# The first layer's input projections by one level of Strassen's scheme

## The chip, the core and the metric

The kernel runs on one core of a Trainium2 chip. The metric is the device time of one execution in microseconds (us). TensorE (PE in the profile) multiplies, with its weight loads (PEld) beside the products; VectorE (DVE), ScalarE (ACT) and GpSimd (POOL) work on elements; SyncE (SP) issues all DMAs of this kernel, in order. Each engine executes its own instructions in program order.

## The reference, cut to what matters

Two layers over 2048 tokens of width 1024. The change touches the first, a stick-breaking attention layer with 16 heads of 64:

```python
proj = rms_norm(x, norm_g) @ w_in          # (2048 x 1024) @ (1024 x 4096)
q, k, v, gate = jnp.split(proj, 4, axis=-1)
# per block of 128 queries:
z = q . k * scale
log_fail = where(mask, log_sigmoid(-z), 0)
later = reverse_cumsum(log_fail) - log_fail
a = where(mask, exp(log_sigmoid(z) + later), 0)
o = a @ v
x = x + (o * silu(gate)) @ w_out
```

The second layer is latent attention with a softmax; nothing of it is changed. Products are in single precision: every operand is split into a high part (as the matmul reads it) and the rest, and three products of parts (`HLS`) stand for one.

## The kernel before

**Stages of layer one.** The work goes by head pairs (`hp`, 8 of them) and, within one, by token groups (`j`, 4 of 512 tokens): 32 stages. `proj0(n)` projects stage n; `attn0(hp, j)` is its attention. The program writes `attn0` of a stage and then `proj0` of the next, whose priorities are spread over the attention's, so that the products of the next stage fill PE's waits of this one.

**A projection** has four units (q, k, v, gate), each 128 outputs by 512 tokens in one PSUM bank (`pj`): 8 blocks of 128 inputs times 3 products of parts, so 24 matmuls of 512 columns, 96 for a stage. Activations come as tiles `xn` (512 KB, high and low part), loaded from the scratch `xn_d` in every pair but the first; in the first, the normed x is turned on PE, scaled by the gain, split and written there (`norm_scale`, `norm_turn`). Weights (`w`, high and low) stay for the four stages of a pair; in the last one each unit's successor is loaded in pieces (`wraw`) and split by ACT and POOL (`load_w`). Then q is split into `qd`, k into `ks`, v is copied, turned and split into `vv`, and the gate becomes `gt`.

**Attention** goes head by head (2 in a pair), over key groups g = j to 0, and over 4 row tiles of 128 queries. A row tile is: 2 matmuls into `z`, two sigmoids on ACT, a scan on DVE (`pp`), a product on POOL (`a`), up to 4 turns on PE (`t`), the split into `at` by ACT and DVE (a subtraction), and 2 matmuls of `av` on average. So DVE has one scan and one subtraction in each row tile, POOL one product and small copies. Where g = j, a row tile has 128 to 512 keys; elsewhere 512. Rings: 3 banks for z, 3 buffers for pp, 5 for a.

**What sets the order.** A list scheduler in the program (`Sched.issue`) places each engine's instructions by modelled durations, then by priority; the order on each engine is fixed from then on. The chip only waits where an operand is late.

Of the kernel before, what the change touches and what calls it, by code (L numbers as in the profile page):

```python
# [11 lines left out]
F32 = mybir.dt.float32  # L12
# [370 lines left out]

@with_exitstack
def trunk(ctx: ExitStack, tc: tile.TileContext, x, w0, wo0, g0, g1, wlat, wgate, gqa, gkva,
# [23 lines left out]
    xn_d = scratch([NG, KD, P, 2, G], "xn_d")  # L409
    y_d = scratch([NG, P, HP0, 2, G], "y_d")  # L410
# [60 lines left out]

    def norm_turn(xts, gain, dst, j, tag=None):
# [28 lines left out]
    XB = KD + 2  # L501
    ws, kv, xq, cur = {}, {}, {}, {}

    def load_w(hp, u, early=None):
        w = pw.tile([P, 2, KD, P], F32R, "w", 4)
        for n, raw in enumerate(early or ()):
            k = slice(4 * n, 4 * n + 4)
            split_sb(w[:, 0, k], w[:, 1, k], raw, 4 * P, "dve" if n else "pool")
        if early:
            ws[hp, u] = w  # L510
            return
        for k in range(0, KD, 2):
            raw = pw.tile([P, 2, P], F32, "wraw", 4)
            C.dma(raw, w0[hp, u, :, k:k + 2, :], 128)
            split_sb(w[:, 0, k:k + 2], w[:, 1, k:k + 2], raw, 2 * P)
        ws[hp, u] = w

    def xn_tile():
        return pw.tile([P, 2, G], F32R, "xn", XB)

    def load_xn(hp, j, k):
        t = xn_tile()
        C.dma(t.all().bitcast(F32), xn_d[j, k], 512)
        xq[hp, j, k] = t

    def load_x(j):
        if j < 2:
            xt = pa.tile([P, 4, D], F32, "at", 2)
            xts = [xt[:, i, :] for i in range(4)]
        else:  # L530
            xts = [pk.tile([P, D], F32, ("ks", "vv")[i % 2], 5).all() for i in range(4)]
        for i in range(4):
            C.dma(xts[i], x[(4 * j + i) * P:(4 * j + i + 1) * P, :], 512)
        return xts

    def xn_dst(j):
        def dst(k):
            xq[0, j, k] = xn_tile()
            return xq[0, j, k]
        return dst  # L540

    stages = [(hp, j) for hp in range(HP0) for j in range(NG)]

    def proj0(n):
        hp, j = stages[n]
        nxt = stages[n + 1] if n + 1 < len(stages) else None

        def mul(u, after=None):
            acc = bank("pj")
            w = ws[hp, u]  # L550
            unit(acc, lambda a, k: w[:, a, k, :], lambda k, b: xq[hp, j, k][:, b, :], after=after)
            if j == NG - 1 and hp + 1 < HP0:
                load_w(hp + 1, u)
            return acc

        acc = mul(0)
        qd = pk.tile([P, 2, 2, G], F32R, "qd", 2)
        for h in range(2):
            lo_, hi_ = slice(64 * h, 64 * h + 64), slice(64 - 64 * h, 128 - 64 * h)
            split(qd[lo_, h, 0, :], qd[lo_, h, 1, :], acc[lo_, :])  # L560
            C.dma(qd[hi_, h].bitcast(F32), qd[lo_, h].bitcast(F32), 256)
        acc = mul(1)
        ks = pk.tile([P, 2, G], F32R, "ks", 5)
        for h in range(2):
            lo_, hi_ = slice(64 * h, 64 * h + 64), slice(64 - 64 * h, 128 - 64 * h)
            split(ks[lo_, h, :], ks[hi_, h, :], acc[lo_, :])
        acc = mul(2)
        vt = pa.tile([P, G], F32, "tmp", 2)
        C.act(vt, acc, AF.Copy)
        tb = bank("pj")  # L570
        with sched.group():
            for c in range(4):
                C.turn(tb[:, c * P:(c + 1) * P], vt[:, c * P:(c + 1) * P], ident)
# [3 lines left out]

        def ahead(k):
            if nxt and nxt[0] > 0:
                if k == 0:  # L580
                    for e in range(XB - KD):
                        load_xn(*nxt, e)
                if k + XB - KD < KD:
                    load_xn(*nxt, k + XB - KD)

        acc = mul(3, ahead)
        sg = pa.tile([P, G], F32, "tmp", 2)
# [59 lines left out]
    x0 = load_x(0)  # L647
    C.dma(gsb0, g0, 4)
    C.dma(gsb1, g1, 4)
    load_w(0, 0)  # L650
    early = {}
    for u in range(1, 4):
        early[u] = []
        for n in range(2):
            if u < 3:
# [3 lines left out]
            raw = raw.rearrange("p (k d) -> p k d", k=4)  # L659
            C.dma(raw, w0[0, u, :, 4 * n:4 * n + 4, :], 256)  # L660
            early[u].append(raw)
    nextx = load_x(1) if NG > 1 else None
    norm_scale(pa, x0, "tmp", 2, True)
    norm_turn(x0, gsb0, xn_dst(0), 0)
    C.fill(later[:, 0:G - P], 0.0)
    causal(later[:, G - P:G], -1, 1.0)
    for u in range(1, 4):
        load_w(0, u, early[u])
    if NG > 1:
        norm_scale(pa, nextx, "tmp", 2)  # L670
    proj0(0)
# [20 lines left out]
    for n, (hp, j) in enumerate(stages):  # L692
# [3 lines left out]
        if n + 1 < len(stages):  # L696
            if hp == 0 and j + 1 < NG:
                norm_turn(nextx, gsb0, xn_dst(j + 1), j + 1, "pj")
            proj0(n + 1)
            late = len(sched.ops)  # L700
            if hp == 0 and j + 2 < NG:
                nextx = load_x(j + 2)
                norm_scale(pa, nextx, "tmp", 2)
# [457 lines left out]
```

## Time and profile before

| | us |
|---|---|
| median of 3 runs (3061.26 to 3068.74) | 3061.82 |
| the profiled execution | 3061.58 |
| its span, first to last instruction | 3059.9 |
| layer one: first row tile to the end of its attention | 39 to 1588 |
| one pair in the regular part (second to seventh) | 187.0 |

A span's busy shares are means over very different stretches. The regular part of layer one repeats itself with 187.0 us from pair to pair, so that one pair can be read for six. Busy time of PE counts matmuls that overlap in the pipeline; what a matmul costs in a row of them is the distance of starts. The same holds on DVE: its instructions of 512 columns follow one another some 80 ns sooner than their ends say.

### The profile page before, as it was taken

What the parts mean: (1) busy time and instruction counts of PE and PEld (TensorE: products, weight loads), DVE (VectorE), ACT (ScalarE), POOL (GpSimd) and SP (SyncE); (2) the same over time, 40 slices, a digit from 0 to 9 for tenths busy, and PEclk for the clock granted to TensorE, in tenths of its full rate; (3) what the DMA queues carried; (4) which work ended last, traced back from release to release, by engine and by line L of the source; (5) the groups of instructions that cost most, each with busy time, mean ns of one, the idle gap of its engine ahead of it and who ended that gap; (6) DMA issues with size and microseconds to landing.
All of it is one profiled execution on the core that took longest, in us unless ns stands there. A gap on an engine that the chain in (4) does not pass through costs nothing.

```text
span 3059.9 us, 48542 instructions
## 1 busy us (share of the span) xinstructions
PE 2978.5 (97%) x15728; PEld 2486.1 (81%) x15728; DVE 2024.9 (66%) x3553; ACT 1865.3 (61%) x4635; POOL 1491.4 (49%) x2931
## 2 busy tenths in 40 slices
PE   8899999999999999999999999999999999999999
PEld 6678888888888888888778888878888888888787
DVE  5777896978868778787863231047778777778511
ACT  5676786867768677786852132247777776777400
POOL 4664664756647565574652120136456455555200
PEclk9899999999999999999999999999999999999999
DMA  6253334344243342433339673142222232223462
GB/s 241 104 172 124 130 105 140 109 138 148 81 152 103 125 152 83 150 112 115 126 122 324 243 274 117 69 158 83 78 92 72 86 104 66 75 78 93 160 219 103
DMA packets 134797, 399.87 MB, mean 131 GB/s; under 512 B 16656, under 2 KB 39696, under 8 KB 131984
## 3 DMA queue, kind: packets, MB, share of 16 engines
q1 hardware_dynamic: 134544, 396.76, 38.3%
q8 instruction: 126, 2.06, 0.3%
q14 instruction: 127, 1.04, 0.1%
HBM read 272.97 MB, written 98.57 MB: 121 GB/s over the span
## 4 chain that ended last, share of the span: by engine, by line
PE 75%; DVE 11%; ACT 7%; issue 3%; POOL 2%; DMA 2%; POOLq 0%; DVEq 0%; ACTq 0%; SPq 0%
PE pj L297 30%; PE z L297 21%; PE av L297 12%; PE t L301 9%; DVE pp L342 3%; PE t L297 3%; DVE at L319 1%; DVE pt L319 1%; PE pj L301 1%; ACT s L312 1%; ACT a L312 1%; DVE qs L329 1%; DVE y L319 1%; DVE nm L349 1%; ACT j L312 1%
## 5 line engine op out<-in xcount | busy, mean ns | idle before, releaser
L297 PE MATMUL pj<-xn,w 128*128 128x512 f32 x3072 | 863.6, 402 | 2.0 <-DVE qd L319 1.9
L319 POOL TENSOR_TENSOR a<-a,pp 128x512 f32<-128x512 f32 (+3 forms) x640 | 611.6, 958 | 474.0 <-DVE pp L342 437.4
L297 PEld LDWEIGHTS pj<-xn,w 128*128 128x128 f32 x3072 | 545.4, 188 | 100.0 <-issue 3.7
L342 DVE TENSOR_TENSOR_SCAN pp<-z,cy,a 128x512 f32<-128x512 f32 x384 | 484.1, 1273 | 43.8 <-ACT z L312 39.8
L312 ACT ACTIVATE at<-t 128x512 fp32r<-128x512 f32 (+3 forms) x640 | 340.8, 535 | 156.7 <-PE t L301 154.6
L319 DVE TENSOR_TENSOR at<-t,at 128x512 fp32r<-128x512 f32 (+3 forms) x640 | 377.8, 599 | 84.4 <-ACT at L312 79.5
L312 ACT ACTIVATE a<-z 128x512 f32<-128x512 f32 (+3 forms) x640 | 335.5, 535 | 115.7 <-PE z L297 93.0
L297 PE MATMUL z<-ks,qd 128*128 128x512 f32 (+3 forms) x1280 | 365.2, 377 | 13.7 <-DVE pp L342 9.0
L297 PE MATMUL av<-at,vv 128*128 128x512 f32 (+3 forms) x1280 | 376.1, 379 | 2.1 <-DVE at L319 2.1
L301 PE MATMUL t<-ident,a 128*128 128x128 f32 x2176 | 343.6, 274 | 8.9 <-POOL a L319 4.3
L301 PEld LDWEIGHTS t<-ident,a 128*128 128x128 f32 x2176 | 271.6, 141 | 83.3 <-POOL a L319 7.9
L312 ACT ACTIVATE z<-z 128x512 f32<-128x512 f32 (+3 forms) x640 | 338.7, 536 | 0.7
L329 POOL TENSOR_SCALAR s<-s,c,ri 128x512 f32<-128x512 f32 (+3 forms) x280 | 200.9, 729 | 172.9 <-DVE ri L360 128.1
L297 PEld LDWEIGHTS z<-ks,qd 128*128 128x128 f32 x1280 | 225.2, 190 | 66.6 <-DVE pp L342 20.9
L297 PE MATMUL av<-pt,vv 128*128 128x512 f32 (+2 forms) x960 | 266.3, 384 | 5.0 <-DVE pt L319 3.9
L297 PE MATMUL z<-knt,qn 128*128 128x512 f32 (+2 forms) x960 | 256.8, 376 | 12.1 <-ACT s L312 11.8
L312 ACT ACTIVATE s<-z,nm 128x512 f32<-128x512 f32 (+2 forms) x320 | 199.8, 627 | 102.7 <-DVE nm L349 68.0
L297 PEld LDWEIGHTS av<-at,vv 128*128 128x128 f32 x1280 | 223.1, 190 | 38.0 <-DVE at L319 5.5
L319 DVE TENSOR_TENSOR pt<-t,pt 128x512 fp32r<-128x512 f32 (+1 forms) x312 | 184.3, 606 | 98.6 <-ACT pt L312 96.5
L342 DVE TENSOR_TENSOR_SCAN pp<-z,later 128x128 f32<-128x128 f32 (+3 forms) x256 | 204.3, 814 | 46.8 <-ACT z L312 28.5
L312 ACT ACTIVATE pt<-t 128x512 fp32r<-128x512 f32 (+1 forms) x312 | 163.3, 536 | 72.6 <-PE t L301 70.3
L297 PEld LDWEIGHTS z<-knt,qn 128*128 128x128 f32 x960 | 160.4, 189 | 35.8 <-ACT s L312 17.9
(234 smaller groups left out, 4945.5 us busy)
## 6 DMA issues: line engine op xcount, KB each, us to landing
xn<-xn_d SPq DMA_DIRECT2D x224, 512.0 KB, 4.7
xn_d<-xn SPq DMA_DIRECT2D x64, 512.0 KB, 3.8
y_d<-yh SPq DMA_DIRECT2D x64, 512.0 KB, 2.6
y<-y_d SPq DMA_DIRECT2D x60, 512.0 KB, 5.1
qd<-qd SPq DMA_DIRECT2D x64, 256.0 KB, 3.1
xk<-xn_d SPq DMA_DIRECT2D x32, 512.0 KB, 6.1
cqt<-c_d SPq DMA_DIRECT2D x16, 1024.0 KB, 5.0
ckv<-c_d SPq DMA_DIRECT2D x32, 512.0 KB, 3.7
```

The lines of the kernel that those rows point to most:

```text
L297: lambda: self.nc.tensor.matmul(R(out), lhsT=R(l), rhs=R(r), start=start, stop=stop),
L301: self.s.add("pe", 109.0, lambda: self.nc.tensor.transpose(R(out), R(src), R(ident)), refs(out), refs(src, ident))
L312: self.nc.scalar.activation(R(out), R(src), func, **kw)
L319: self.s.add(eng, ns, lambda: self.eng[eng].tensor_tensor(out=R(out), in0=R(a), in1=R(b), op=op), refs(out), refs(a, b))
L329: self.s.add(eng, ns, lambda: self.eng[eng].tensor_scalar(out=R(out), in0=R(a), scalar1=R(s1), scalar2=R(s2), op0=op0, op1=op1), refs(out) ...
L342: lambda: self.nc.vector.tensor_tensor_scan(R(out), R(a), R(b), initial=R(init), op0=ALU.mult, op1=op),
L349: lambda: self.nc.vector.tensor_reduce(out=R(out), in_=R(src), axis=AX.X, op=op, **kw),
```

## The change

One level of Strassen's scheme, in its form with seven products (Winograd's), on blocks: the 1024 inputs are halved, the 512 tokens of a group are halved, and of the four units two pairs are formed (q with k, v with gate), of which each pair's two units are the halves of the outputs. Of eight products of blocks, seven are left, each with 512 inputs, 128 outputs and 256 tokens; both unit pairs share a PSUM bank. A stage has 7 x 4 x 2 x 3 = 168 matmuls of 256 columns.

- Weights: seven combinations for each unit pair (`WB`), four of them sums or differences. In the first pair they are formed by DVE and POOL (`first_w`); for the later ones `load_w` loads the raw blocks for each combination anew (56 pieces of 128 KB where 16 were), forms the sums on POOL, and splits 28 pieces where it split 16.
- Activations: seven combinations (`XBL`) of two 512 KB tiles (`xs`), so 14 where 8 were. In the first pair they are summed by POOL and DVE (`make_x`), turned, split and written to `xs_d`; in the later ones they are loaded, through a ring of 4 (`XB`, before 10).
- Gain: multiplied onto x in its rows (`gain_scale`), so that it needs a row of gains over all partitions, made at the start; before, it was a scale in the split.
- Results: the products are summed from PSUM into `c1` and `c2` in SBUF: one ACT copy and seven DVE sums a stage. `qd` and `ks` are then split from there; the product with the gate's sigmoid goes from DVE to POOL.

```diff
-    XB = KD + 2
+    XB = 4
+    H = G // 2
+    PAIR = ((0, 1), (2, 3))
...
+    def load_w(hp, s):
+        for p, (ua, ub) in enumerate(PAIR):
+            w = w_tile()
+            for n in range(2):
...
+                b = WB[s]
+                if b[0] == "A":
+                    t = raw(b)
+                else:
+                    t = raw("A21") if b != "S3" else raw("A11")
+                    other = raw("A22") if b != "S3" else raw("A21")
+                    C.tt("pool", t, t, other, ALU.add if b != "S3" else ALU.subtract, H)
+                    if b in ("S2", "S4"):
+                        C.tt("pool", t, t, raw("A11"), ALU.subtract, H)
+                    if b == "S4":
+                        C.tt("pool", t, raw("A12"), t, ALU.subtract, H)
+                split_sb(w[:, 0, ks_], w[:, 1, ks_], t, 2 * P)
...
+    def gain_scale(pl, xts, grow, mixed=False):
...
+            if mixed and i % 2 == 0:
+                C.act(xts[i], xts[i], AF.Copy, D, scale=r)
+                C.tt("pool", xts[i], xts[i], grow, ALU.mult, D)
+            else:
+                C.stt(xts[i], xts[i], r, grow, ALU.mult, ALU.mult, D)
...
+        for s in range(7):
+            if hp == 0:
+                make_x(j, s, xh)
             acc = bank("pj")
...
+                        for p in range(2):
+                            for m, (a, b) in enumerate(HLS):
+                                C.mm(acc[:, p * H:(p + 1) * H], ws[hp, p, s][:, a, k, :], xt[:, kk, b, :],
+                                     k == 0 and m == 0 and p == 0, k == 3 and m == 2 and p == 1, H)
             if j == NG - 1 and hp + 1 < HP0:
-                load_w(hp + 1, u)
+                load_w(hp + 1, s)
+            if s == 0:
+                C.act(c1[:, :, 1, :], av_, AF.Copy)
+            elif s == 1:
+                C.tt("dve", c1[:, :, 0, :], av_, c1[:, :, 1, :], ALU.add)
...
-        C.act(sg, acc, AF.Sigmoid)
         gt = pa.tile([P, G], F32, "gt", 2)
-        C.tt("dve", gt, acc, sg, ALU.mult)
+        C.act(gt, g_, AF.Sigmoid)
+        C.tt("pool", gt, g_, gt, ALU.mult)
```

**How the order moves.** PE, in the attention of the fifth pair's last token group, shortly after its first key groups. `pj<-xn,w` (`pj<-xs,w` in the changed kernel) are matmuls of the next projection, `z`, `t` and `av` those of the attention. Before:

```order
L297 MATMUL z<-ks,qd 128x512 x2
L297 MATMUL pj<-xn,w 128x512 x6
L301 MATMUL t<-ident,a 128x128 x4
L297 MATMUL z<-ks,qd 128x512 x2
L297 MATMUL pj<-xn,w 128x512 x3
L301 MATMUL t<-ident,a 128x128 x4
L297 MATMUL z<-ks,qd 128x512 x2
L297 MATMUL pj<-xn,w 128x512 x3
```

And in the changed kernel, at the same row tiles:

```order
L301 MATMUL t<-ident,a 128x128 x8
L297 MATMUL z<-ks,qd 128x512 x2
L297 MATMUL av<-at,vv 128x512 x4
L301 MATMUL t<-ident,a 128x128 x4
L297 MATMUL av<-at,vv 128x512 x2
L297 MATMUL z<-ks,qd 128x512 x2
L297 MATMUL av<-at,vv 128x512 x2
L301 MATMUL t<-ident,a 128x128 x4
```

Before, three or six projection matmuls stand between any two row tiles. In the changed kernel there is none from the 57th to the 79th of that pair's 80 row tiles (46 matmuls of z): the projection that could fill stands complete ahead of them.

POOL, in the fifth pair's third token group, where the weights of the next pair are made: `a<-a,pp` is a row tile's product, `w<-wraw,w` the split of a weight piece, `wraw<-wraw` a sum of two. Before:

```order
L319 TENSOR_TENSOR w<-wraw,w 128x256 x2
L319 TENSOR_TENSOR a<-a,pp 128x512
L364 COPY cy<-pp 128x1
L364 COPY pp<-cy 128x1
L364 COPY cy<-pp 128x1
L319 TENSOR_TENSOR a<-a,pp 128x512
```

And in the changed kernel:

```order
L319 TENSOR_TENSOR w<-wraw,w 128x256 x2
L364 COPY pp<-cy 128x1
L364 COPY cy<-pp 128x1
L319 TENSOR_TENSOR a<-a,pp 128x512
L319 TENSOR_TENSOR wraw<-wraw 128x256
L364 COPY pp<-cy 128x1
L364 COPY cy<-pp 128x1
L319 TENSOR_TENSOR a<-a,pp 128x512
L319 TENSOR_TENSOR wraw<-wraw 128x256 x2
L364 COPY pp<-cy 128x1
```

A row tile's product now has one to three weight instructions behind it; all 56 of a pair stand among the 24 row tiles of the third token group.

DVE, at the start, up to the first scan of the program. `xn` and `xs` are activation splits, `c_` the sums of products, `at` (without `t`) sums of x. Before, 24 instructions stand ahead of the first scan, of which these are the last:

```order
L336 SCALAR_TENSOR_TENSOR tmp,nss<-at 128x1024 x2
L319 TENSOR_TENSOR qd<-pj,qd 64x512 x2
L319 TENSOR_TENSOR ks<-pj,ks 64x512 x2
L319 TENSOR_TENSOR vv<-pj,vv 128x4x128
L336 SCALAR_TENSOR_TENSOR xn<-pj,gsb_91,xn 128x512
L342 SCALAR_TENSOR_TENSOR pp<-z,later 128x128
```

In the changed kernel, 65 instructions stand ahead of it, and its last are:

```order
L319 TENSOR_TENSOR qd<-c_281,qd 64x512 x2
L319 TENSOR_TENSOR vv<-pj,vv 128x4x128
L319 TENSOR_TENSOR c_518<-c_518,pj 128x2x256
L319 TENSOR_TENSOR at<-at 128x512
L319 TENSOR_TENSOR xs<-pj,xs 128x2x256
L319 TENSOR_TENSOR ks<-c_518,ks 64x512 x2
L319 TENSOR_TENSOR tmp<-at 128x512
L319 TENSOR_TENSOR xs<-pj,xs 128x2x256
L342 SCALAR_TENSOR_TENSOR pp<-z,later 128x128
```

Ahead of the first scan stand now 46 element instructions of 512 columns (8 before, and 9 gain splits), 10 of 1024 columns (4 and 2 scalings before) and 8 of 128.

## Rows read from the trace of the kernel before

**Rows 1.** The page: span, then busy us, share and instructions by engine.

```profile
span 3059.9 us, 48542 instructions
PE 2978.5 (97%) x15728; PEld 2486.1 (81%) x15728; DVE 2024.9 (66%) x3553; ACT 1865.3 (61%) x4635; POOL 1491.4 (49%) x2931
```

**Rows 2.** Windows, second and seventh pair: length, busy by engine, clock, DMA.

```profile
277.03:464.05 187.02, 186.35 (x994) 155.00 (x993) 150.26 (x197) 138.97 (x296) 114.85 (x260) 1.00 0.37 125
...
1212.14:1399.20 187.06, 186.44 (x994) 154.99 (x993) 150.59 (x197) 138.93 (x296) 114.85 (x260) 1.00 0.37 122
```

**Rows 3.** Waits, layer one: who for whom, us in all, times, longest.

```profile
POOL a L319 <- DVE pp L342: 437.4, 289, 15.2
```

**Rows 4.** Timeline of PE, 278 to 284: start, us, instructions.

```profile
279.08 3.63 PE L297 MATMUL pj<-xn,w 128*128 128x512 f32 x15
282.55 0.60 PE L301 MATMUL t<-ident,a 128*128 128x128 f32 x4
282.91 0.94 PE L297 MATMUL pj<-xn,w 128*128 128x512 f32 x3
283.69 0.27 PE L301 MATMUL t<-ident,a 128*128 128x128 f32 x1
```

**Rows 5.** Timeline of PE in layer two, where matmuls have 256 columns.

```profile
2136.54 1.59 PE L297 MATMUL pj<-wukv,ckv 128*128 128x256 f32 x12
2137.97 0.45 PE L297 MATMUL z<-knt,qn 128*128 128x128 f32 x3
```

**Rows 6.** Groups of DVE in one pair: count, busy us, mean ns, idle before.

```profile
L319 DVE TENSOR_TENSOR at<-t,at 128x512 fp32r<-128x512 f32 x56 | 37.6, 678 | 6.8 <-ACT at L312 6.4
...
L319 DVE TENSOR_TENSOR y<-y,gt 128x512 f32<-128x512 f32 x4 | 3.1, 768 | 0.0
...
L319 DVE TENSOR_TENSOR gt<-pj,tmp 128x512 f32<-128x512 f32 x4 | 2.7, 683 | 0.0
```

**Rows 7.** Timeline of DVE in the last pair's last token group.

```profile
1538.05 0.66 DVE L319 TENSOR_TENSOR at<-t,at 128x512 fp32r<-128x512 f32 x1
1538.63 1.27 DVE L342 TENSOR_TENSOR_SCAN pp<-z,cy,a 128x512 f32<-128x512 f32 x1
1539.82 0.71 DVE L319 TENSOR_TENSOR wo<-woraw,wo 128x256 fp32r<-128x256 f32 x1
```

**Rows 8.** Windows, the same attention, which has no projection beside it.

```profile
1530.00:1560.00 30.00, 27.58 (x146) 21.55 (x145) 29.47 (x41) 27.41 (x66) 25.62 (x55) 1.00 0.28 85
```

**Rows 9.** Groups of POOL in one pair.

```profile
L319 POOL TENSOR_TENSOR a<-a,pp 128x512 f32<-128x512 f32 x56 | 61.2, 1094 | 35.2 <-DVE pp L342 33.3 <-ACT at L312 1.0 <-ACT a L312 0.3
L319 POOL TENSOR_TENSOR w<-wraw,w 128x256 fp32r<-128x256 f32 x16 | 12.1, 761 | 2.6 <-ACT w L312 2.5
...
L364 POOL COPY cy<-pp 128x1 f32<-128x1 f32 x48 | 8.8, 183 | 2.4 <-DVE pp L342 1.3 <-ACT at L312 1.1
...
L319 POOL TENSOR_TENSOR a<-a,pp 128x256 f32<-128x256 f32 x8 | 5.1, 638 | 12.8 <-DVE pp L342 12.7
```

**Rows 10.** Timeline of DVE at the start.

```profile
5.80 1.23 DVE L336 SCALAR_TENSOR_TENSOR tmp<-at 128x1024 bf16<-128x1024 f32 x1 [5.80 <-DMA at<-in_x_dram]
...
20.01 3.40 DVE L319 TENSOR_TENSOR w<-a,w 128x512 fp32r<-128x512 f32 x2
23.34 0.68 DVE L319 TENSOR_TENSOR w<-pp,w 128x512 fp32r<-128x512 f32 x1
...
39.16 0.75 DVE L336 SCALAR_TENSOR_TENSOR xn<-pj,gsb,xn 128x512 fp32r<-128x512 f32 x1 [1.53 <-ACT xn L312]
40.91 0.42 DVE L342 TENSOR_TENSOR_SCAN pp<-z,later 128x128 f32<-128x128 f32 x1 [1.01 <-ACT z L312]
```

**Rows 11.** Windows, first pair from its first scan, and a stretch in it.

```profile
40.00:262.00 222.00, 208.01 (x1061) 165.93 (x1060) 163.35 (x218) 152.78 (x321) 126.91 (x276) 0.95 0.41 143
...
80.00:90.00 10.00, 4.97 (x15) 2.46 (x14) 8.31 (x11) 8.11 (x18) 9.36 (x16) 0.70 0.13 52
```

**Rows 12.** Loads of xn, 277 to 1399: us from issue to landing.

```profile
DMA to landing us min/median/max: 3.0/4.7/7.2
```

More of the change, by code (lines that the diff above doesn't have):

```diff
@@ L526, in load_x, with xs_tile @@
+    def xs_tile():
+        return pw.tile([P, 2, 2, H], F32R, "xs", XB)
     def load_x(j):
         if j < 2:
[L528 to L531 removed]
+            xt = pa.tile([P, 4, 2, G], F32, "at", 2)
+            halves = [[xt[:, i, h, :] for h in range(2)] for i in range(4)]
+            whole = [xt[:, i].rearrange("p a b -> p (a b)") for i in range(4)]
+        else:
+            tiles = [pk.tile([P, 2, G], F32, ("ks", "vv")[i % 2], 5) for i in range(4)]
+            halves = [[t[:, h, :] for h in range(2)] for t in tiles]
+            whole = [t.all().rearrange("p a b -> p (a b)") for t in tiles]
@@ L532, in load_x @@
         for i in range(4):
[L533 to L540, printed above, removed]
-    stages = [(hp, j) for hp in range(HP0) for j in range(NG)]
-    def proj0(n):
-        hp, j = stages[n]
-        nxt = stages[n + 1] if n + 1 < len(stages) else None
-        def mul(u, after=None):
-            acc = bank("pj")
-            w = ws[hp, u]
-            unit(acc, lambda a, k: w[:, a, k, :], lambda k, b: xq[hp, j, k][:, b, :], after=after)
-            if j == NG - 1 and hp + 1 < HP0:
-                load_w(hp + 1, u)
[L554 to L562, printed above, removed]
+            C.dma(whole[i], x[(4 * j + i) * P:(4 * j + i + 1) * P, :], 512)
@@ new lines, in load_x, with make_x @@
+        return whole, halves
+    t2s = {}
+    def make_x(j, s, xh):
+        b = XBL[s]
+        eng = ("pool", "dve")
+        if b == "T2":
+            for i in range(2):
+                C.tt(eng[i], xh[i][0], xh[i + 2][0], xh[i][0], ALU.subtract)
+                t2s[i] = pa.tile([P, G], F32, "tmp", 2)
+                C.tt(eng[i], t2s[i], xh[i + 2][1], xh[i][0], ALU.subtract)
+        elif b == "T3":
+            for i in range(2):
+                C.tt(eng[i], xh[i + 2][0], xh[i + 2][1], xh[i + 2][0], ALU.subtract)
+        elif b == "T4":
+            for i in range(2):
+                C.tt(eng[i], xh[i][1], t2s[i], xh[i][1], ALU.subtract)
+        src = {"B11": lambda i: xh[i][0], "B21": lambda i: xh[i][1], "B22": lambda i: xh[i + 2][1],
+               "T1": lambda i: xh[i][0], "T2": lambda i: t2s[i][:, :], "T3": lambda i: xh[i + 2][0],
+               "T4": lambda i: xh[i][1]}[b]
+        for hb in range(2):
+            tb = bank("pj" if j else ("z", "t", "z", "t", "z", "av")[(2 * s + hb) % 6])
+            with sched.group():
+                for kk in range(2):
+                    for i in range(2):
+                        k, o = 2 * hb + kk, (2 * kk + i) * P
+                        C.turn(tb[:, o:o + P], src(i)[:, k * P:(k + 1) * P], ident)
+            t = xs_tile()
+            split(t[:, :, 0, :], t[:, :, 1, :], tb.all().rearrange("p (k t) -> p k t", k=2))
+            C.dma(xs_d[j, 2 * s + hb], t.all().bitcast(F32), 512)
+            xq[j, 2 * s + hb] = t
@@ L576, in proj0 @@
         split(vv[:, :, 0::3, :], vv[:, :, 1:3, :], tv)
[L578 to L587, printed above, removed]
-        C.act(sg, acc, AF.Sigmoid)
         gt = pa.tile([P, G], F32, "gt", 2)
-        C.tt("dve", gt, acc, sg, ALU.mult)
+        g_ = c2[:, 1].rearrange("p a t -> p (a t)")
+        C.act(gt, g_, AF.Sigmoid)
+        C.tt("pool", gt, g_, gt, ALU.mult)
         kv[hp, j] = (ks, vv)
```

155 lines of the change are left out of this document (111 added, 44 removed).

## The prediction

> **What bounds the kernel now.** The page first: PE is busy 97% of the span, DVE 66%, ACT 61%, POOL 49% [rows 1]. Those are means, so the windows come next: layer one repeats with 187.0 us a pair, in which PE is busy 186.4, DVE 150.3 to 150.6, ACT 139 and POOL 114.9, at a full clock [rows 2]. PE is the limit there, and DVE has only 36 us to spare in a pair. The waits say the same from the other side: POOL waits 437 us for DVE's scans [rows 3], the longest of all in layer one, and PE's sums are small beside that. But where attention has no projection beside it, the limit is another: in the last pair's last token group DVE is busy 29.5 of 30 us and PE 27.6 by its modelled ends [rows 8]. So a projection does two things here: it costs PE time, and it fills the time in which attention waits for DVE. What the change saves is worth something only while both hold.
>
> **Fewer columns on PE.** Fifteen matmuls of 512 columns take 282.55 - 279.08 = 3.47 us, 0.231 each [rows 4]; twelve of 256 columns in a row take 1.43, 0.119 each [rows 5], so half the columns cost 52%, weight loads included. A stage had 96 x 0.231 = 22.2 us and has 168 x 0.119 = 20.0: 2.2 less, 8.6 in a pair, 69 in 32 stages. With PE alone a pair would take 187.0 - 8.6 = 178.4.
>
> **Work added to DVE.** A pair gets 28 sums from PSUM and loses 4 gate products. A subtraction of 512 columns is followed by the next instruction after 0.58 [rows 7], and the gate product (one operand in PSUM, one in SBUF, as the new sums) lasts as long as a subtraction, 683 against 678 ns [rows 6]. So 24 x 0.6 = 14.4: DVE rises from 150.5 to 165, 92% of 178.4. That would still fit if it were spread evenly. It isn't. In the last token group's attention the new order has 23 row tiles (57th to 79th) with no projection matmul between them. Of their 22 intervals, 18 are of 512 keys and 4 on the diagonal (128 to 512 keys, mean 320). DVE needs 0.58 + 1.19 = 1.77 for a scan and a subtraction [rows 7]: 18 x 1.77 + 4 x 1.77 x 320/512 + 2 x 0.6 (for y) = 37.5. PE needs for such a row tile 4 matmuls and 4 turns. A turn is (283.69 - 282.55 - 3 x 0.231)/4 = 0.11 [rows 4], so a row tile is 1.36, and the stretch 18 x 1.36 + 4 x 0.85 = 27.9. PE waits for 9.6; less some 1.6 for the row tile by which it can lead with three banks of z: 8. Its bounds are 5 (a lead of three row tiles) and 10. So 178.4 + 8 = 186.4: nearly the whole saving is given back to DVE.
>
> **Work added to POOL.** In a pair, 12 more weight splits at 0.76, 28 sums of 256 columns, for which the product of 256 columns at 0.64 is the nearest row, and 4 gate products at 1.09 [rows 9]: 9.1 + 17.9 + 4.4 = 31, so 114.9 becomes 146, 82% of 178. All 56 weight instructions stand among the third token group's 24 row tiles, so POOL has there 28 x 0.76 + 28 x 0.64 = 39 and, with 16 full row tiles at 1.09 + 2 x 0.18 [rows 9] and 8 shorter ones at some 0.9, 30 for attention, 69 in all. PE has in the same stretch 24 row tiles (28 us) and one and a half projections (31): 59. Of the 10 more, POOL may lag three row tiles (three buffers of pp), and it has slack before and after. I take 1.5; bounds 0 and 7.
>
> **Loads.** xs comes 14 times a stage where xn came 8 times, and wraw 56 times a pair where it came 16: at 122 to 125 GB/s [rows 2], 23.3 MB a pair become 41, 220 GB/s, more than any regular pair had. The lead is shorter: with 4 buffers, three tiles of 12 matmuls each are 3 x 1.43 = 4.3 us where products stand close, and a load took 3.0 to 7.2, median 4.7 [rows 12]. Mixed with attention the lead doubles. I take 1 us a pair; bounds 0 and 5. So a regular pair is 186.4 + 1.5 + 1 = 189, against 187: 2 more, six times, +12. ACT, at 139 [rows 2], gets 12 short splits and one copy in place of another, under 40 us of slack: nothing.
>
> **The last pair** makes no weights, and its last attention was bound by DVE before too [rows 8]. It keeps the 8.6, less 2.6 where DVE's sums now reach PE's time in the third token group: -6 (bounds -9 and 0).
>
> **The first pair** is where most is added. DVE has up to the second pair's first scan 109 more element instructions of 512 columns (42 more activation splits and sums of x and of weights among them), 14 more of 1024, and 32 gain splits less: 109 x 0.6 + 14 x 1.15 - 32 x 0.66 = +60, less a little: 181 before, 241 now. Before, it was done at 262, with 59 of the 222 us after the first scan idle [rows 11]. Ahead of the first scan, DVE now has 46 x 0.6 + 10 x 1.15 + 8 x 0.2 = 41 where 17 were. x lands at 5.8, and the first scan was at 40.9 with 18 us of waits [rows 10]; 5.8 + 41 + 11 of waits puts it at 58, +17. Behind it, 163.4 + 36 = 200 of work; with some 32 idle (half of the former 59) that is 232 against 222, +10. Together +27. Bounds: with no wait at all 5.8 + 241 = 247, 16 earlier than before; with all former waits +60. I take the middle, a little up, for the reason in the next paragraph. PE's own additions there (24 more turns a stage and 8 for the gains, 11 us) are covered by this wait; uncovered, they eat its saving.
>
> One thing makes the start worse than a count of instructions. Two DVE weight splits took 3.40 us together while POOL ran its own, and a third 0.68 with POOL between instructions [rows 10]; such splits read both operands from SBUF. The Trainium skill has a rule for it ("SBUF — State Buffer", section "SBUF: two separate sides"): VectorE with two SBUF inputs and GpSimd take one shared port pair by an exclusive lock, and the loser waits for the whole instruction. The trace agrees in those two splits, and less elsewhere: y<-y,gt, of that kind too, took 768 on average against 678 [rows 6]. The rule speaks against this change, which adds such operations on both engines. By the rows' 0.09, the 16 splits of q and k a pair, now from SBUF, cost 1.4, inside DVE's waits above; by the rule taken at its word, half a POOL instruction of 1.09 or so for each of them, the sum is near that of the last rival, which is priced from rows alone.
>
> **Sum.** Against the profiled execution's 3061.6 (span 3059.9, median of the runs 3061.8, so they agree): +27 for the first pair, +12 for the regular ones, -6 for the last: 3094.6, **3095 us**. Layer two is not touched: 0.
>
> **Rivals.**
> - *PE's saving arrives* (17%). PE fills its waits in the stretch without projection more than I count, because DVE runs ahead through the second half of each pair. For it: DVE's total stays below PE's, and PE was never idle. Against it: 0.98 of DVE's time was busy in the row tiles without a projection, and PE did wait there. Time: 69 saved less the first pair's 27, 3061.6 - 69 + 27 = 3020; with half the loss per pair, 3045.
> - *It comes out even* (14%). DVE and POOL give back just what PE gains in the regular pairs (0 where I have +12), and the start costs 10 or so: 3061.6 + 10 - 6 = 3066.
> - *DVE and POOL block each other* (15%). Every q and k split from SBUF (16 in a pair) meets a POOL instruction and pays half of the start's 1.70 - 0.68: 8 us a pair on the engine that now sets the pace, six times. 3095 + 48 = 3143. It decides from about 3 us a pair on. For it: POOL at 82%. Against it: the 768 above.
> - That the products don't become cheaper is excluded as far as runs of twelve go [rows 5].
>
> **Chances.** Forecast 54%, the rivals 17, 14 and 15%. No change is within 0.3%, 9 us, about what a measurement of this kernel can tell. The forecast and the lock lie above it (69%), the even case in it but for 2 points (12%), the first rival and those 2 below (19%). The range goes from 3040, with part of the first rival inside, to 3145, with the lock inside; low end: bounds of DVE's loss (5), no POOL or DMA cost and a start at 0; high end: the upper bounds of half the terms.
>
> **What the profile will show.** Right if: xs matmuls at 0.12 apart; a regular pair of 187 to 191; in its last token group DVE busy over 95% and PE waiting before z for DVE's pp; DVE near 165 and POOL near 146 a pair; the first scan near 58, the second pair's first near 289. Wrong if a pair takes under 183 (DVE's loss is not there), if PE waits chiefly for xs loads or for w, or if the first pair ends no later than 262.

## The result, and the profile after

The changed kernel takes 3267.7 us (median of 4 runs, 3264.0 to 3272.4) against 3061.7 before (3061.3 to 3068.7): a ratio of 1.067, 95% interval 1.0645 to 1.0691. It is 206 us slower. The prediction had slower, by 33; the time lies above its range.

The page of the changed kernel, to be read against [rows 1]: span, busy time of each engine, then two groups of layer one's projections and of the new sums (busy us, mean ns, idle before and its releaser).

```profile
span 3270.7 us, 55223 instructions
PE 3023.4 (92%) x18136; PEld 2601.9 (80%) x18136; DVE 2235.9 (68%) x3813; ACT 1918.8 (59%) x4749; POOL 1803.7 (55%) x3254
...
L297 PE MATMUL pj<-xs,w 128*128 128x256 f32 x5376 | 789.4, 291 | 64.1 <-DVE c L319 44.0
...
L319 DVE TENSOR_TENSOR c<-pj,c 128x512 f32<-128x512 f32 x192 | 128.6, 683 | 89.1 <-PE pj L297 66.4
```

PE has fewer columns to do, and yet its share fell from 97 to 92%: it waits now. By these means no engine has become full in its place; DVE is at 68% and POOL at 55%. Means over the span hide what single stretches show, as will be seen for POOL. The new operations have the durations that were counted (683 ns for a sum).

Where the 211 us of span came from is read from the start of the first z matmul of each pair in the two traces:

| stretch | before | after | difference | predicted |
|---|---|---|---|---|
| start to the first z | 39.0 | 78.1 | +39 | +17 |
| first pair | 223.6 | 256.9 | +33 | +10 |
| six regular pairs | 1124.0 | 1251.9 | +128 (208.7 for 187.3 each) | +12 |
| last pair, to its last av | 201.1 | 205.3 | +4 | -6 |
| layer two | 1472.2 | 1478.4 | +6 | 0 |

Three fifths of the loss is in the regular pairs. Windows of one of them, by token group and as a whole, with the columns of [rows 2]:

```profile
959.10:992.50 33.40, 30.51 (x232) 28.44 (x230) 26.09 (x39) 16.59 (x37) 15.97 (x33) 1.00 0.73 237
992.50:1030.80 38.30, 38.16 (x289) 36.23 (x289) 30.61 (x42) 26.29 (x56) 20.54 (x48) 1.00 0.65 220
1030.80:1093.20 62.40, 59.44 (x433) 54.94 (x431) 48.84 (x63) 44.19 (x98) 56.85 (x105) 1.00 0.87 282
1093.20:1167.20 74.00, 60.92 (x335) 46.14 (x333) 62.45 (x78) 56.62 (x119) 59.01 (x121) 0.93 0.31 98
959.10:1167.20 208.10, 189.04 (x1282) 165.74 (x1280) 167.99 (x221) 143.69 (x309) 152.36 (x305) 0.98 0.61 198
```

Busy totals came out close to the forecast: DVE 168 where 165 was counted, POOL 152 where 146 was. What did not come out is the pair's length: 208 where 189 was predicted. Most of the loss is in the third and fourth token groups (62.4 for 53.8 and 74.0 for 63.3 before). The third has POOL busy 57 of 62; the fourth has DVE busy 62 of 74, PE only 61, and a mean clock of 0.93.

These windows go by the first z on PE. At that moment POOL still has products and weight work of the group before in front of it. So here is the third token group by POOL's own marks, from its first attention product to the first of the fourth group, after and then before:

```profile
1034.90:1111.90 77.00, 67.99 (x464) 61.19 (x463) 54.40 (x70) 49.17 (x110) 70.94 (x130) 0.93 0.80 257
898.60:954.50 55.90, 55.59 (x298) 46.13 (x297) 46.40 (x60) 46.06 (x103) 42.45 (x92) 1.00 0.48 158
```

By these marks the third group takes 77.3 for 55.9 (mean of the six regular pairs), 21 more, which is the whole loss of a pair; the other three groups together take 131.2 for 131.4. POOL is busy 71 of the 77. In the rest it waits mostly for raw weights (3.6) and for ACT's parts of the splits (2.1), and never for one of DVE's scans. So in this stretch POOL has become the limit, at 92%. In the fourth group DVE is busy 58.2 of 60.7, at 96%, and PE 54.7.

The seam of the two is the worst place. Windows of 5 us there:

```profile
1096.80:1101.80 5.00, 3.62 (x20) 2.18 (x19) 3.37 (x5) 2.81 (x7) 5.00 (x9) 0.99 0.54 183
...
1103.00:1108.00 5.00, 0.50 (x3) 0.05 (x1) 1.46 (x3) 2.86 (x9) 4.66 (x8) 0.50 0.52 162
1108.00:1113.00 5.00, 5.00 (x27) 5.00 (x28) 2.17 (x3) 0.23 (x1) 5.00 (x12) 0.61 0.47 144
```

And the timeline of POOL in them, then of DVE and of PE (start, us, what ended the idle time before):

```profile
1100.30 1.09 POOL L319 TENSOR_TENSOR a<-a,pp 128x512 f32<-128x512 f32 x1
1101.35 2.79 POOL L319 TENSOR_TENSOR wraw<-wraw 128x256 f32<-128x256 f32 x4
...
1105.90 1.26 POOL L319 TENSOR_TENSOR gt<-c,gt 128x512 f32<-128x512 f32 x1
1107.23 2.81 POOL L319 TENSOR_TENSOR w<-wraw,w 128x256 fp32r<-128x256 f32 x4
1109.97 1.11 POOL L319 TENSOR_TENSOR a<-a,pp 128x512 f32<-128x512 f32 x1
```

```profile
1107.20 2.01 DVE L319 TENSOR_TENSOR c<-pj,c 128x512 f32<-128x512 f32 x3 [3.44 <-POOL gt L319]
1111.12 0.96 DVE L342 TENSOR_TENSOR_SCAN pp<-z,later 128x384 f32<-128x384 f32 x1 [1.90 <-POOL a L319]
```

```profile
1102.26 1.19 PE L297 MATMUL z<-ks,qd 128*128 128x512 f32 x2
1107.95 5.22 PE L297 MATMUL pj<-xs,w 128*128 128x256 f32 x27 [4.50 <-DVE c L319]
```

Between two attention products POOL works off weight sums and splits and the gate product for 8.6 us, almost without a gap. DVE's sums need c, which POOL's gate product still reads; PE's next projection needs the pj bank that those sums read, and stands for 4.5 us. In the middle window every engine but POOL is idle more than 40% of the time. The granted clock falls to 0.50, the lower level of 1.2 GHz, at 1101.7, when PE had been busy 3.62 of the last 5.00 us and before its stand of 4.5 us, and is back at 1111.9. So the low level outlasts the stand, and the 27 matmuls behind it take 5.22 us. Drops of 3.4 to 10.2 us come in each regular pair here; in the pairs before, the clock was 1.00 throughout [rows 2].

The waits of the whole run say the same of all pairs, against [rows 3]:

```profile
POOL a L319 <- DVE pp L342: 288.6, 251, 8.7
...
PEld t L301 <- POOL a L319: 84.6, 113, 4.2
...
PE pj L297 <- DVE c L319: 44.0, 25, 5.9
PE t L301 <- POOL a L319: 44.0, 64, 4.0
...
DVE pp L342 <- POOL a L319: 32.7, 33, 2.7
```

POOL waits 149 us less for DVE, and PE now waits for POOL's products. If PE's matmuls are taken at their spacing before (0.231 for 512 columns, three quarters of it for 384, 0.119 for 256 [rows 4, 5], turns and others of 128 at 0.11), the pair at 959 needs 176.3 us of PE, where a pair before needs 185.0 by the same count. The 8.7 saved are there; 32 us of waits, of overlaps in their wake and of the lower clock came on top, where before there were 2.

The start is another matter. DVE's timeline there, against [rows 10]:

```profile
6.29 1.23 DVE L336 SCALAR_TENSOR_TENSOR tmp<-at 128x1024 bf16<-128x1024 f32 x1 [2.13 <-DMA at<-in_x_dram]
...
10.39 3.37 DVE L336 SCALAR_TENSOR_TENSOR tmp<-at 128x1024 bf16<-128x1024 f32 x1
...
20.94 0.68 DVE L319 TENSOR_TENSOR xs<-z,xs 128x512 fp32r<-128x512 f32 x1
...
28.25 1.78 DVE L319 TENSOR_TENSOR a<-a 128x512 f32<-128x512 f32 x1
...
36.47 3.42 DVE L319 TENSOR_TENSOR w<-pp,w 128x512 fp32r<-128x512 f32 x2
...
81.03 0.99 DVE L342 TENSOR_TENSOR_SCAN pp<-z,later 128x128 f32<-128x128 f32 x2
```

The first scan is at 81.0 where 58 was predicted. Operations with one operand in PSUM take 0.68 (xs<-z,xs); those with both in SBUF take 0.68 where POOL is idle or at something small, and mostly 1.7 to 1.8 otherwise, and an activation square of 1024 takes 3.37 in place of 1.23. To 78 us DVE is busy 60 where 41 was counted.

### The profile page after: what moved, and what is told of

Read it like the earlier page. It is cut to its first block, busy times and chain, and to the rows that moved or that the text cites. A ratio compares the mean times of both kernels' runs of the same rounds, so it can differ in the third digit from the quotient of the medians.

```text
span 3270.7 us, 55223 instructions
## 1 busy us (share of the span) xinstructions
PE 3023.4 (92%) x18136; PEld 2601.9 (80%) x18136; DVE 2235.9 (68%) x3813; ACT 1918.8 (59%) x4749; POOL 1803.7 (55%) x3254
## 3 DMA queue, kind: packets, MB, share of 16 engines
q14 instruction: 140, 1.15, 0.1%
## 4 chain that ended last, share of the span: by engine, by line
PE 56%; DVE 16%; POOL 8%; ACT 7%; issue 6%; DMA 6%; POOLq 0%; SPq 0%; ACTq 0%; DVEq 0%
PE pj L297 22%; PE z L297 17%; PE av L297 8%; PE t L301 6%; DVE pp L342 5%; DVE at L319 3%; POOL a L319 3%; PE t L297 2%; DMA wraw<-in_w_dram 2%; POOL wraw L319 2%; ACT a L312 1%; DMA qd<-qd 1%; ACT z L312 1%; DVE pt L319 1%; POOL w L319 1%
## 5 line engine op out<-in xcount | busy, mean ns | idle before, releaser
L297 PE MATMUL pj<-xs,w 128*128 128x256 f32 x5376 | 789.4, 291 | 64.1 <-DVE c L319 44.0
L297 PEld LDWEIGHTS pj<-xs,w 128*128 128x128 f32 x5376 | 715.8, 194 | 104.8 <-DVE c L319 51.4
L319 POOL TENSOR_TENSOR a<-a,pp 128x512 f32<-128x512 f32 (+3 forms) x640 | 622.1, 973 | 311.4 <-DVE pp L342 288.6
L297 PE MATMUL z<-ks,qd 128*128 128x512 f32 (+3 forms) x1280 | 391.1, 391 | 51.8 <-DVE pp L342 25.1
L301 PE MATMUL t<-ident,a 128*128 128x128 f32 x2176 | 353.8, 279 | 50.6 <-POOL a L319 44.0
L301 PEld LDWEIGHTS t<-ident,a 128*128 128x128 f32 x2176 | 260.5, 142 | 122.4 <-POOL a L319 84.6
L297 PEld LDWEIGHTS z<-ks,qd 128*128 128x128 f32 x1280 | 206.0, 194 | 103.5 <-DVE pp L342 38.1
L297 PEld LDWEIGHTS av<-at,vv 128*128 128x128 f32 x1280 | 213.6, 192 | 31.8 <-DVE at L319 11.8
L312 ACT ACTIVATE pt<-t 128x512 fp32r<-128x512 f32 (+1 forms) x312 | 163.2, 536 | 72.4 <-PE t L301 70.4
L319 DVE TENSOR_TENSOR c<-pj,c 128x512 f32<-128x512 f32 x192 | 128.6, 683 | 89.1 <-PE pj L297 66.4
```

What stands on the lines that cost most here:

```text
L297: lambda: self.nc.tensor.matmul(R(out), lhsT=R(l), rhs=R(r), start=start, stop=stop),
L301: self.s.add("pe", 109.0, lambda: self.nc.tensor.transpose(R(out), R(src), R(ident)), refs(out), refs(src, ident))
L312: self.nc.scalar.activation(R(out), R(src), func, **kw)
L319: self.s.add(eng, ns, lambda: self.eng[eng].tensor_tensor(out=R(out), in0=R(a), in1=R(b), op=op), refs(out), refs(a, b))
```

## The experiments

All of them are read by the length of the six regular pairs (first z to first z, mean of six; 187.3 before, 208.7 after), by the first z of the program (39.0, 78.1) and by the whole time. The kernel before took 3060.3 to 3066.2 beside them. Each was one run, which is enough for differences of some us a pair; the two runs that change only the start have regular pairs of 209.1 and 209.6, so a difference of 1 or 2 us says little.

**Is it the weight work on POOL?**

```diff
-                    C.tt("pool", t, t, other, ALU.add if b != "S3" else ALU.subtract, H)
...
-                        C.tt("pool", t, t, raw("A11"), ALU.subtract, H)
+                        raw("A11")
...
-                        C.tt("pool", t, raw("A12"), t, ALU.subtract, H)
+                        raw("A12")
```

> The changed kernel with POOL's 28 weight sums of each later pair left out (each combination takes one of its blocks; all loads stay), so the projections of pairs two to eight are not those of the reference. Theory A (POOL's weight instructions, standing ahead of the attention's products, cost the 21 us a pair): with 28 x 0.72 = 20 us less on POOL in the third token group a pair takes 188 to 193, the whole 3145 to 3185. Theory B (DVE's 28 sums a pair are the loss): a pair stays at 205 to 208, the whole above 3245. Theory C (the gate product on POOL blocks DVE): 198 to 208.

Measured: 192.9 a pair, 15.8 less; 3166.4 us. One pair as a window:

```profile
902.30:1094.50 192.20, 182.51 (x1282) 164.11 (x1281) 168.20 (x221) 144.13 (x309) 133.08 (x277) 1.00 0.67 214
```

POOL is busy 19 less, DVE as long as in the changed kernel, and the clock is at 1.00: in four of the six pairs the drop of the clock goes too (191.7 to 192.7 us each), in two a drop of 3.4 us stays (194.0 and 194.6). 19 us of POOL's work, on an engine that had more than 50 to spare in the pair, cost 16. By POOL's marks the third group falls from 77.3 to 56.2, nearly what it was before the change, and the fourth rises from 60.8 to 66.7. All loads are still there (214 GB/s in this window), so the loads as such are not what these 16 us are.

**Is it the gate product, moved from DVE to POOL?**

```diff
-        C.tt("pool", gt, g_, gt, ALU.mult)
+        C.tt("dve", gt, g_, gt, ALU.mult)
```

> The changed kernel with the gate product back on DVE. Theory C (DVE's next sum waits for the gate product that stands behind POOL's weight work, and holds DVE's scans and PE): a pair falls to 195 to 200, the whole to about 3190. Theory A: POOL still has its 56 weight instructions in the third token group; a pair at 203 to 208, the whole 3235 to 3270. Theory B: DVE has 2.4 us more a pair, 208 to 211.

Measured: 206.6 a pair, 2.1 less; 3257.1. The product is what DVE waits for in the timeline above, but it is one of eleven operations between the two attention products: without it the other ten are still there. A small part, hardly clear of the scatter between runs.

**Is it DVE's sums?**

```diff
-            elif s == 2:
-                C.tt("dve", c1[:, :, 1, :], av_, c1[:, :, 1, :], ALU.add)
...
-                C.tt("dve", c1[:, :, 1, :], av_, c1[:, :, 1, :], ALU.add)
-            elif s == 5:
-                C.tt("dve", c1[:, :, 1, :], av_, c1[:, :, 1, :], ALU.add)
-            else:
-                C.tt("dve", c2[:, :, 0, :], c2[:, :, 0, :], av_, ALU.subtract)
```

> The changed kernel with four of DVE's seven sums of products a stage left out (the results of these products are not added), 16 x 0.6 = 9.6 us of DVE a pair. Theory B: a pair falls by 8 to 12, to 196 to 200, the whole to about 3190. Theory A: the third token group and the start of the fourth stay as they are; the fourth gets shorter by no more than the sums that lie in it: 203 to 208, the whole above 3230.

Measured: 199.0 a pair, 9.7 less, for 9.6 us of DVE's work by count (16 x 0.6); 3182.8. The first z came at 70.4. So DVE's part is as real as POOL's, and the two theories are not rivals but both hold. Not all of the 9.7 need be DVE's own time, though: a sum that is left out also frees its PSUM bank sooner, and PE's waits for the sums fell from 38.1 to 15.3 us over the six pairs, 3.8 a pair. No run separates the two.

**Both left out.** The weight sums on POOL and these four sums of DVE:

> The changed kernel with both left out: POOL's 28 weight sums a pair and four of DVE's seven sums of products a stage. If the two costs are separate pieces of one chain (POOL's in the third token group, DVE's in the rest), their effects add: 208 - 15.5 - 9.9 = 183 a pair, near the 178 that PE alone would need, the whole about 3085. If they are the same wait seen twice, little is added to the first: 190 to 193, the whole about 3150. At 183 the first pair alone would keep it slower than before.

Measured: 185.8 a pair, 22.9 less (15.8 and 9.7 make 25.5, so they nearly add); 3099.6. One pair:

```profile
871.00:1056.60 185.60, 180.81 (x1282) 166.50 (x1282) 157.45 (x205) 143.19 (x309) 131.96 (x277) 0.99 0.70 222
```

Even with 30 us of work a pair left out, a pair is only 1.5 shorter than before, and the start (70.0) and the first pair (240.0) cost more than six such pairs give. Most of the price is in doing the sums at all, not in how they are arranged. Not every added microsecond costs the same, though: the 30 us taken out were worth 23, while the 24 that are left (7 on DVE, 17 on POOL) cost 7, the distance from the 178.6 that PE's saving alone would give.

**Is it the order?** First by the scheduler's durations, set to the trace's:

```diff
-        self.s.add("pe", max(n / 2.4, 107.0) + 3.0,
+        self.s.add("pe", max(0.4375 * n + 8.0, 109.0),
...
-        ns = 70.0 + 1.045 * n if eng == "dve" else 155.0 + 2.1 * n
+        ns = 70.0 + 1.045 * n if eng == "dve" else 340.0 + 1.37 * n
```

> The changed kernel, complete, with the list scheduler's durations set to those of the trace (matmuls of 512, 256 columns 0.232, 0.120; POOL's products of 512 columns 1.04). Theory order (the fixed order was made with durations that POOL and PE don't keep, so engines wait where the plan saw no wait): a pair falls to 195 to 200, the whole to about 3190. Theory work (the instructions themselves, wherever the planner puts them within the third token group): 204 to 208, the whole 3245 to 3270.

Measured: 210.8 a pair, 3324.0 in all, of which 30 more lie in layer two, whose order the durations set as well. Worse, not better. Then by the place of the weight work, spread into the fourth token group:

```diff
+    wops = []
...
+                wops.extend(sched.ops[i0:])
...
+        if j == NG - 1 and wops:
+            for i, o in enumerate(wops):
+                o.prio = a0 + 0.6 * (a1 - a0) * i / len(wops)
+            wops.clear()
```

> The changed kernel, complete, with the weight work of the next pair ranked among the fourth token group's attention in place of the third's: by the new order 21 of 56 weight instructions stand in the third group, 35 in the fourth, and projection matmuls stand between nearly all row tiles of the fourth. Theory position (POOL's weight instructions cost because they stand close together and ahead of products, and leave the fourth group without filler): a pair falls to 188 to 195, the whole to 3120 to 3170. Theory amount (POOL's and DVE's added time as such): it stays above 203, the whole above 3235.

Measured: 206.9 a pair, 3250.7. The pair at 951:

```profile
951.00:1158.10 207.10, 190.62 (x1281) 169.48 (x1280) 168.89 (x221) 144.28 (x308) 151.00 (x305) 0.97 0.63 198
```

Place is worth 1.8 of the 21. POOL is at 73% over the whole pair, DVE at 82%; the longest stretch of weight work between two products is 4.0 us, where it was 8.6, and PE still waits. By POOL's marks the long stretch has moved with the work: the third group takes 54.8, the fourth 77.1 for 60.8 (means of six). The fourth in this pair:

```profile
1086.10:1162.80 76.70, 70.10 (x448) 59.02 (x447) 62.57 (x77) 56.29 (x120) 68.74 (x133) 0.98 0.62 196
```

**Too few buffers?** A fourth pp buffer needs room, so it has a control of its own, with three xs buffers and one of woraw:

```diff
-    XB = 4
+    XB = 3
...
-            load_wo(pm, wo0, 0, KD, G // 2, 3)
+            load_wo(pm, wo0, 0, KD, G // 2, 1)
```

> The control for the next run: the changed kernel with three buffers of xs in place of four and one of woraw in place of three; nothing else. What is open: with the weight work spread over two token groups a pair still took 207, though no engine was full. Theory R (too few buffers of pp between DVE's scans and POOL's products, so that each engine is held by the other) and theory Q (PE takes its instructions in one fixed order, and a turn that waits for a product holds everything behind it, however many buffers there are) both expect no more than the loss by shorter loads here: pairs of 208 to 212, 3270 to 3290 in all, and PE's waits for xs at 0.7 to 4 us a pair.

> The control with a fourth buffer of pp, for which it made room. Theory R (buffers): POOL may lag one row tile more, DVE's waits for POOL (33 in all) mostly go, and a pair gets shorter by 4 to 10 us against the control: 198 to 205, some 30 to 70 in all. Theory Q (fixed order): DVE's waits for POOL shrink, but PE's turns wait for products as before (129 in all for PE and its weight loads), and a pair stays within 2 us of the control.

Measured: 218.5 for the control (3392.0 in all), 216.8 with four pp (3372.7); layer two, which has one woraw for three as well, grew by 58 to 60 in both. The control cost more a pair than expected, 9.9: with three buffers the loads are late, but PE's waits for xs are only 3.5 a pair (21.2 over the six), and where the rest comes from was not found. The fourth pp buffer gave 1.7. The waits of the control, then of the run with four:

```profile
PEld t L301 <- POOL a L319: 76.5, 93, 4.2
...
PE pj L297 <- DMA xs<-xs_d: 25.3, 27, 2.7
```

```profile
PEld t L301 <- POOL a L319: 80.7, 102, 4.2
PEld z L297 <- DVE pp L342: 80.6, 121, 2.6
```

PE's turns wait for products as before: buffers of pp are not it. Those of the products (`a`) and the PSUM banks of the projection were not varied. So the order was tried a third way, with a longer delay between a POOL result and its reader, and beside it five buffers of xs:

```diff
-    LAT = {"pe": 120.0, "act": 120.0, "dve": 180.0, "pool": 150.0, "sp": 2000.0}
+    LAT = {"pe": 120.0, "act": 120.0, "dve": 180.0, "pool": 650.0, "sp": 2000.0}
```

> The changed kernel, but the scheduler that writes out each engine's order counts 0.65 us instead of 0.15 between a POOL result and its reader, so that PE's turns stand later behind other PE work. A fourth buffer of pp gave only 1.6 us a pair, as theory Q (fixed order) wanted. If Q is the cause and the order can mend it, PE's waits for products (129 us in all) fall by more than half and a pair takes 195 to 203, 3160 to 3230 in all. If the work on POOL and DVE itself sets the pace (theory W), the waits only move to z or pj, and a pair stays at 205 to 212, 3250 to 3300.

> The changed kernel with five buffers of xs in place of four, and three of wraw in place of six for room. Three buffers of xs cost 10 us a pair, more than the 0 to 4 expected, while PE's waits for xs were only 0.7 a pair with four. If four were also too few (theory X), a pair gets shorter by 3 to 10 us: 198 to 205. If four are enough, as PE's waits say, a pair takes 207 to 212, with up to 3 more where POOL now waits for wraw; 3265 to 3300 in all.

Measured: 211.1 a pair (3278.6) with the longer delay. The waits of that run:

```profile
PEld z L297 <- DVE pp L342: 90.4, 109, 2.0
PE z L297 <- DVE pp L342: 89.7, 121, 2.5
...
PEld t L301 <- POOL a L319: 33.3, 45, 2.2
PE t L301 <- POOL a L319: 19.3, 31, 2.0
```

The waits for products, of PE and its weight loads together, fell from 129 to 53, as wanted, and came back as waits of z for DVE's scans, 63 in the changed kernel and 180 now. Moving a wait did not remove it. Five xs buffers: 206.7 a pair, 3280.9 (the first pair grew to 271 with fewer wraw); four are about enough. One of its pairs:

```profile
972.40:1179.40 207.00, 186.67 (x1282) 166.43 (x1280) 171.67 (x221) 145.05 (x309) 150.19 (x304) 0.99 0.64 199
```

Here the mean clock is 0.99, against 0.98 and 0.97 above, and a pair is no shorter. The pair from 765.1 has no drop at all and takes 207.3: the clock is not what makes the pairs long.

**The start.** Two theories: that two-operand SBUF work of DVE and POOL shuts each other out, or that there is simply too much of it for DVE. First, all of POOL's element work there given to DVE:

```diff
-        dp, pd = ("dve", "pool"), ("pool", "dve")
+        dp, pd = ("dve", "dve"), ("dve", "dve")
...
-        eng = ("pool", "dve")
+        eng = ("dve", "dve")
...
-    gain_scale(pa, x0, grow, True)
+    gain_scale(pa, x0, grow)
```

> The changed kernel with POOL's element work of the start and of the first pair's activations (x times gain, weight sums and splits of the first pair, sums of x) moved to DVE. Theory L (two-operand work of DVE and POOL excludes one another, so that it takes turns whichever engine has it): the first row tile stays within 5 us of 78, or earlier; single DVE instructions of 512 columns fall from 1.7 to 0.7 us. Theory N (the number of instructions on each engine is the cost): some 25 instructions more on DVE, 15 to 20 us more, the first row tile at 93 to 98. The pairs behind the first stay at 208 by both.

Measured: the first z at 74.1, 4 us earlier; 3270.8 in all. The first 78 us, of the changed kernel and of this one:

```profile
0.00:78.00 78.00, 41.27 (x260) 37.19 (x260) 59.96 (x66) 30.50 (x51) 46.91 (x49) 0.82 0.54 200
```

```profile
0.00:78.00 78.00, 41.88 (x283) 38.38 (x284) 56.00 (x89) 31.35 (x56) 17.37 (x33) 1.00 0.55 206
```

With POOL down from 47 to 17, DVE did 89 operations in 56 us, where it did 66 in 60. Its timeline has the same kinds of work at their undisturbed price, for instance three splits in 1.89:

```profile
24.44 1.89 DVE L319 TENSOR_TENSOR w<-a,w 128x512 fp32r<-128x512 f32 x3
```

Shared work between the two engines gains nothing at the start, as they hardly overlap in it. The Trainium skill's rule ("SBUF — State Buffer", section "SBUF: two separate sides": one port pair by an exclusive lock) fits this run and the 1.7 us above. The clock is at 1.00 here and was 0.82, and the first z comes only 4 us sooner, so the start was not slow by the clock either.

Second, no sums of x and of the first weights:

```diff
-        add(3, 2, 3, ALU.add, pd)
-        add(2, 0, 2, ALU.subtract, dp)
-        add(0, 3, 0, ALU.subtract, pd)
...
-        add(1, 1, 0, ALU.subtract, pd)
...
-        if b == "T2":
...
+               "T1": lambda i: xh[i][0], "T2": lambda i: xh[i][0], "T3": lambda i: xh[i + 2][0],
```

> The changed kernel with all sums of x and the sums of the first pair's weights left out (splits, gains and turns stay; the first pair's weight and activation combinations are then single blocks). Up to the first row tile these are 8 sums of weights and at least 8 of x. Theory L (DVE and POOL exclude one another with two operands from SBUF): each costs 1.7 or so to both: 16 x 1.0 to 1.7, the first row tile at 52 to 62. Theory N (count by engine): 8 x 0.6 on DVE or 8 x 1.1 on POOL, the first row tile at 68 to 72. Pairs two to eight stay at 208.

Measured: the first z at 65.6, between the two expectations, 3247.1 in all. It doesn't tell them apart. It does show that 12.5 of the 39 us are these sums, and that the larger part (26.6) stays without them.

No version here beats the kernel before: with most of the sums of the regular pairs left out on both engines the scheme was still 36 us slower.

## Why the prediction was wrong

Right: the products. On PE's timeline after, twelve xs matmuls in a row last 1.67 us and six 0.96, so 0.118 for each further one, where 0.119 was read from [rows 5]:

```profile
970.72 1.67 PE L297 MATMUL pj<-xs,w 128*128 128x256 f32 x12
...
972.58 0.96 PE L297 MATMUL pj<-xs,w 128*128 128x256 f32 x6
```

PE's need fell by 8.7 a pair, as the prediction's own figures make it (it wrote 8.6). Right also that PE does not wait for loads with four buffers (under 1 us a pair for xs), though POOL does in its long stretch (3.6 for raw weights), that ACT has slack, and that DVE sets the pace where attention has no projection beside it: at 1135 to 1140 in the fourth token group its scans and subtractions follow each other at 1.77, the price of [rows 7]:

```profile
1135.89 0.66 DVE L319 TENSOR_TENSOR at<-t,at 128x512 fp32r<-128x512 f32 x1
1136.47 1.27 DVE L342 TENSOR_TENSOR_SCAN pp<-z,cy,a 128x512 f32<-128x512 f32 x1
1137.66 0.66 DVE L319 TENSOR_TENSOR at<-t,at 128x512 fp32r<-128x512 f32 x1
```

The 8 us forecast for PE's wait there came out near: in the fourth group by POOL's marks PE is idle 6 of 60.7, though its waits there are put down more to POOL's products (3.4) than to DVE's scans (1.8).

Wrong, in order of size:

- **Work added to POOL: "I take 1.5; bounds 0 and 7".** This is the step that failed. The sums alone cost 15.8 a pair by the run without them, six times. The amount was counted well: 69 us of POOL in the third token group, and it is busy 71 there. The error was to settle the overhang of 10 us over PE's 59 against POOL's slack in the groups before and after, and against three buffers of lag. What the runs show in its place is that POOL sets the length of that stretch: 77 us, its own work and its waits for raw weights and for ACT, where it took 56 before. As the seam shows, a product that comes late delays the turn, then av and z behind it in PE's fixed order, and DVE's next scan, and the fourth group, where DVE is busy 96%, has little to make it good with. Moving the work moved the long stretch with it; another place, a fourth buffer of pp and five buffers of xs each gave 2 us a pair or less, and more delay for the turns gave nothing. Part of the 15.8 is the clock, for which the prediction's sum had no term: of 7 to 10 us a pair at the lower level, four pairs of six without the sums had none. It is a small part, since with the sums kept the one pair without a drop (five xs buffers) still took 207.3.
- **Work added to DVE: 8 a pair.** It was priced only in the stretch without a projection, and the rest was taken to be hidden because 165 is below 178. Sixteen of the 28 sums cost 9.7 a pair, as much as their whole duration, with the PSUM banks that they hold counted in. DVE has 40 us without work in a pair of 208, but not where it sets the pace.
- **The first pair: +17 and +10.** Measured +39 and +33. The count of instructions was right (64 operations counted before the first scan, 66 done in 78 us) and the waits too (11 counted; 78 less 6.3 for x and 60 of work leaves 12). The term that was mis-sized is the price of an operation: 41 us were counted at 0.6 and 1.15, and 60 were used, as POOL worked beside it. That the two engines hold each other up, which the prediction weighed and then priced at 1.4 us a pair and "a little up" for the start, was worth 19 us of DVE's time there. In the regular pairs it is small, though twice the 0.09 that the prediction took from [rows 6]: the splits of q and k, from PSUM in a pair before, and from SBUF in one after (a group's columns as in rows 6):

```profile
L319 DVE TENSOR_TENSOR ks<-pj,ks 64x512 fp32r<-64x512 f32 x8 | 5.5, 689 | 3.8 <-ACT ks L312 3.7
...
L319 DVE TENSOR_TENSOR ks<-c,ks 64x512 fp32r<-64x512 f32 x9 | 7.8, 863 | 0.4
...
L319 DVE TENSOR_TENSOR qd<-c,qd 64x512 fp32r<-64x512 f32 x8 | 7.0, 876 | 0.2
```

  They take about 0.18 more than from PSUM, 3 us in a pair for the 17. The rival that had the two engines block each other at 8 a pair, 48 in all, named a true mechanism at the wrong place.
- **The last pair: -6**, measured +4. It makes no weights and still gives up PE's saving. In the two runs without four of DVE's sums it took 191.2 and 198.4, for 205.3; but with all sums it took 199.7 and 198.6 in the runs with three xs buffers, and 204 to 214 in the others, so whether DVE's sums are the cost there is not shown.

The means of 73 and 82% had suggested cover on both engines. Read by stretches there is little where it counts: POOL is at 92% in the third token group, which holds 23 of DVE's 40 idle us, and DVE at 96% in the fourth, where POOL idles 16. What stays open is how the loss divides between the two. With one engine's sums left out the other's stretch grew (without POOL's, the fourth group took 66.7; without four of DVE's, the third took 83.6). The loop, in which z, scan, product, turn, split and av pass each row tile from PE to DVE to POOL and back in fixed orders, was not tested by a run of its own. Nor was the 6 us in layer two, which the change doesn't touch, looked into; in the runs that change nothing in it, it took 1472.4 to 1478.8, so it may be scatter.

## What to carry to other kernels

When a change takes work from the busiest engine and gives it to two others in the same loop, a sum of each engine's busy time against the busiest one's is not a forecast: here 8.7 us saved on PE came with 17 on DVE and 38 on POOL, all of it "under the slack", and cost 21. Count each engine's work in the stretch where it will stand, by that engine's own marks as here for POOL: where the count exceeds the time that the stretch took before, expect to pay the excess at close to its full duration (here the 30 us taken out gave back 23). Subtract cover only where a row shows it in that stretch. A mean share below 90% is no evidence of cover.

## What the runs showed of the hardware that was not expected

- In a program that keeps PE 92% busy, the granted clock fell to 0.50 in each regular pair, in one after 5 us in which PE was busy 3.62 and had no stand over 1.2 us. It stayed there 10.2 us, also while PE was fully busy again (5.00 of 5.00 us at a mean of 0.61).
- DVE operations on two SBUF operands, 0.68 us by themselves, took 1.7 to 1.8 beside a POOL that was busy with the same kind, and squares of 1024 took 3.37 for 1.23; in steady state, beside a POOL at 73%, the 64-partition splits rose only from 0.69 to 0.87.
- Three load buffers in place of four cost 9.9 us a pair, though with four PE waited for a load under 1 us a pair, and with three 3.5.
